# An encoder trunk in fp32 on one Trainium2 core: the first products behind one turned block of x, every second low part on GpSimd, the first norm's squares on VectorE

## Chip, cores, metric

One core of a Trainium2 chip. The time of a kernel is the device time of one launch in microseconds; three runs of the kernel before were timed, and one more was profiled.

## What is computed

A two-layer encoder trunk on 256 tokens of width 1024, fp32. Each layer adds half a SwiGLU block, a mixer (attention of two kinds in the even layer, neighbourhood attention in the odd one) and another half SwiGLU block, each behind an RMS norm:

```python
def rms_norm(x, g):
    y = x * lax.rsqrt(jnp.mean(x * x, axis=-1, keepdims=True) + EPS)
    return y * g
def swiglu(h, w_gate, w_up, w_down):
    return (jax.nn.silu(h @ w_gate) * (h @ w_up)) @ w_down
for layer in range(2):
    x = x + 0.5 * swiglu(rms_norm(x, ffn1_norm[layer]), ffn1_w_gate[layer], ...)
    x = x + mixer(rms_norm(x, mix_norm[layer]), ...)
    x = x + 0.5 * swiglu(rms_norm(x, ffn2_norm[layer]), ffn2_w_gate[layer], ...)
return rms_norm(x, final_norm)
```

The change touches only the very first of these products, `h @ w_gate` on its first 512 columns, and the norm ahead of it.

## The kernel before

The 256 tokens are two tiles (`tt` 0 and 1) of 128 rows. A product needs x turned, so that its width lies on the partitions: eight blocks of 128 columns (`k` 0 to 7) for each tile. Every fp32 operand of a product is split into a high part (rounded to the matmul's format, made by ScalarE) and a low part (what the rounding left, made by VectorE), and a product is three matmuls: high by high, low by high, high by low (`mm`, L407 to L409). For the turned x the two parts are `th` (`part_h`, L447) and `tl` (`part_l`, L452), with the norm's gain on them. For weights they are `hi` (`high_part`, L415) and `lo` (`low_part`, L418). The norm's other factor, one number per row, is applied later, in silu and in the product with the up branch.

Weights are loaded by SyncE's queue into `raw` tiles. `supply` takes the next piece, issues its high part, and keeps its low part back until `low`, at the next `tick` or `supply`. Each product of three matmuls ends in a `tick`, which also steps the spawned tasks (each counts ticks until its next step) and adds `rate` to `due`; when `due` reaches a piece's size, another `supply` is issued ahead of need. The order on every engine is the order in which this program issues, by hand.

The opening is `first_gates`. Four matmuls of zeros warm TensorE (`WARM`). `turn(j)` transposes blocks 2j and 2j + 1 of both tiles into two PSUM banks, `parts(j, banks)` makes their parts and those of the weights, two products' worth of weights (`FIRST`: pieces of 1, 1, 2, 2 and 2 blocks). After `turn(0)` two more matmuls of zeros follow (`FILL`), and then `turn(1)` and its parts stand ahead of the first product:

```python
        parts(0, turn(0))
        for _ in range(FILL):
            self.warm()
        ...
        for j in range(KD // 2):
            if j + 1 < KD // 2:
                banks = turn(j + 1)
                parts(j + 1, banks)
            for k in (2 * j, 2 * j + 1):
                for tt in range(NT):
                    self.mm(ps[tt], now.hT[tt][k], W[k], k == 0, k == KD - 1)
```

`row_rstd`, one task for each tile, squares the two halves of a row on ScalarE with a running sum (L436), adds them on VectorE (L439), scales (L425) and takes the power -1/2 on GpSimd (L427). `SQ_WAIT` is the number of ticks before each starts. The second silu (L594) waits for the second tile's power.

The loads, on SyncE's queue: `mats` (identity and gains), weight block 0, x columns 256 to 512 of both tiles, weight block 1, weight blocks 2 and 3, x columns 512 to 1024, weight blocks 4 to 7; x columns 0 to 256 go through ScalarE's queue.

## Time and profile before

| | us |
|---|---|
| three timed runs: median (lowest, highest) | 966.1 (964.84, 966.28) |
| the profiled execution | 964.81 |
| its span | 963.0 |
| TensorE busy | 950.6 |
| VectorE busy | 694.9 |
| ScalarE busy | 558.0 |
| GpSimd busy | 89.2 |

The span is what the profiler records between the first and the last instruction; the time has 1.8 us more around it. An engine's busy time counts its instructions, so what TensorE lacks to the span is where it stood. The chain that ended last, followed back from the last instruction, says which work set the end.

### The profile page before, as it was taken

Reading aid. Unit: us, or ns where it says so; the run is one execution under the profiler, and the core shown is the slowest. Engines: PE = TensorE matmul, PEld = TensorE weight load, DVE = VectorE, ACT = ScalarE, POOL = GpSimd, SP = SyncE. Lnnn points to the kernel's source line nnn. Section 1 sums busy time; section 2 is a strip of 40 time slices with the busy share of each in tenths; the row PEclk is TensorE's granted clock in tenths of the full one; section 3 lists DMA queues with packets and bytes.
Section 4 is the critical chain, followed back from the end, with each engine's and each line's share of the span. In section 5 each row is a group of like instructions: output and inputs, shape, how many; then the busy total and the mean of one; then the engine's idle time right before and its main releaser. Section 6 shows DMA issues by size and latency. Waiting matters only on the chain.

```text
span 963.0 us, 12839 instructions
## 1 busy us (share of the span) xinstructions
PE 950.6 (99%) x4803; PEld 803.8 (83%) x4803; DVE 694.9 (72%) x1103; ACT 558.0 (58%) x967; POOL 89.2 (9%) x152
## 2 busy tenths in 40 slices
PE   9999999999999999999999999999999999999997
PEld 6888998877878888988888899888878888889886
DVE  6665679778866655787866558889877776655987
ACT  7554556477776545565554445447877575545551
POOL 1030000063420000000000000005130000000001
PEclk9999999999999999999999999999999999999999
DMA  8665565643425744755456556563634356555642
GB/s 285 195 238 185 175 219 178 216 132 89 131 88 201 235 154 131 240 217 207 149 192 207 174 161 220 191 243 132 187 113 135 129 195 201 188 152 182 208 172 80
DMA packets 82367, 171.64 MB, mean 178 GB/s; under 512 B 3712, under 2 KB 25216, under 8 KB 82304
## 3 DMA queue, kind: packets, MB, share of 16 engines
q1 hardware_dynamic: 81728, 170.23, 53.9%
q8 instruction: 37, 0.61, 0.3%
q10 hardware_dynamic: 576, 0.59, 0.2%
q14 instruction: 26, 0.21, 0.1%
HBM read 169.76 MB, written 1.05 MB: 177 GB/s over the span
## 4 chain that ended last, share of the span: by engine, by line
PE 91%; DVE 4%; ACT 2%; POOL 1%; issue 1%; DMA 1%; POOLq 0%; ACTq 0%; DVEq 0%
PE pj L407 14%; PE pj L409 14%; PE pj L408 14%; PE s L409 12%; PE s L407 12%; PE s L408 11%; PE tp L484 3%; PE o L815 2%; PE o L408 1%; PE o L409 1%; PE o L407 1%; PE tp L894 1%; DVE lo L418 1%; PE tp L462 1%; PE s L830 1%
## 5 line engine op out<-in xcount | busy, mean ns | idle before, releaser
L418 DVE TENSOR_TENSOR lo<-raw,hi 128x1024 fp32r<-128x1024 f32 (+2 forms) x388 | 383.2, 1011 | 122.5 <-ACT hi L415 119.0
L415 ACT ACTIVATE hi<-raw 128x1024 fp32r<-128x1024 f32 (+2 forms) x388 | 328.0, 877 | 150.2 <-PE pj L409 101.7
L407 PE MATMUL pj<-hi,th 128*128 128x512 f32 (+1 forms) x512 | 198.1, 387 | 0.0
L409 PE MATMUL pj<-hi,tl 128*128 128x512 f32 (+1 forms) x512 | 192.9, 377 | 0.0
L408 PE MATMUL pj<-lo,th 128*128 128x512 f32 (+1 forms) x512 | 192.7, 376 | 0.1
L407 PE MATMUL s<-hi,th 128*128 128x512 f32 (+1 forms) x400 | 152.2, 380 | 0.0
L409 PE MATMUL s<-hi,tl 128*128 128x512 f32 (+1 forms) x400 | 149.4, 373 | 0.0
L408 PE MATMUL s<-lo,th 128*128 128x512 f32 (+1 forms) x400 | 149.0, 373 | 0.0
L409 PEld LDWEIGHTS pj<-hi,tl 128*128 128x128 f32 x512 | 96.1, 188 | 15.5
L407 PEld LDWEIGHTS pj<-hi,th 128*128 128x128 f32 x512 | 96.4, 188 | 13.8 <-issue 0.9
L408 PEld LDWEIGHTS pj<-lo,th 128*128 128x128 f32 x512 | 96.4, 188 | 13.4 <-DVE lo L418 0.5
L409 PEld LDWEIGHTS s<-hi,tl 128*128 128x128 f32 x400 | 75.2, 188 | 11.0
L408 PEld LDWEIGHTS s<-lo,th 128*128 128x128 f32 x400 | 75.4, 189 | 10.4
L407 PEld LDWEIGHTS s<-hi,th 128*128 128x128 f32 x400 | 75.5, 189 | 10.2
L599 DVE SCALAR_TENSOR_TENSOR glu<-pj,rstd,silu 128x512 f32<-128x512 f32 (+1 forms) x48 | 33.6, 701 | 36.8 <-PE pj L409 36.6
L418 DVE TENSOR_TENSOR g_l<-tp,g_h 128x384 fp32r<-128x384 f32 (+1 forms) x48 | 29.0, 604 | 22.4 <-ACT g_h L415 22.4
L427 POOL TENSOR_TENSOR rstd<-var,mhalf 128x1 f32<-128x1 f32 (+2 forms) x16 | 15.2, 949 | 311.2 <-DVE var L425 311.1
L407 PE MATMUL s<-hi,g_h 128*128 128x512 f32 (+1 forms) x108 | 42.8, 396 | 0.0
L415 ACT ACTIVATE g_h<-tp 128x384 fp32r<-128x384 f32 (+1 forms) x48 | 25.3, 526 | 29.1 <-PE tp L484 19.0
L409 PE MATMUL s<-hi,g_l 128*128 128x512 f32 (+1 forms) x108 | 42.0, 389 | 0.0
L408 PE MATMUL s<-lo,g_h 128*128 128x512 f32 (+1 forms) x108 | 41.9, 388 | 0.0
L447 ACT ACTIVATE th<-tp,mats 128x128 fp32r<-128x128 f32 x88 | 25.1, 371 | 28.4 <-PE tp L462 25.8
(381 smaller groups left out, 1382.0 us busy)
## 6 DMA issues: line engine op xcount, KB each, us to landing
raw<-in_ffn_w_down SPq DMA_DIRECT2D x44, 1024.0 KB, 5.0
raw<-in_ffn_w_up SPq DMA_DIRECT2D x32, 1024.0 KB, 5.2
raw<-in_ffn_w_gate SPq DMA_DIRECT2D x30, 1024.0 KB, 5.3
raw<-in_ffn_w_gate SPq DMA_DIRECT2D x16, 768.0 KB, 4.5
raw<-in_ffn_w_up SPq DMA_DIRECT2D x16, 768.0 KB, 4.8
raw<-in_odd_w_qkv SPq DMA_DIRECT2D x12, 1024.0 KB, 5.3
raw<-in_even_w_in SPq DMA_DIRECT2D x4, 1024.0 KB, 5.2
raw<-in_even_w_out SPq DMA_DIRECT2D x8, 512.0 KB, 5.8
```

What stands on the lines that cost most here:

```text
L407: mm(ps, h, wh, start=first, stop=False)
L408: mm(ps, h, wl, start=False, stop=False)
L409: mm(ps, l, wh, start=False, stop=last)
L415: self.nc.scalar.activation(hi, src, AF.Copy)
L418: self.nc.vector.tensor_tensor(lo, src, hi.bitcast(F32), op=ALU.subtract)
L427: nc.gpsimd.tensor_tensor(r[:, :n], v[:, :n], self.mhalf[:, :n], op=ALU.pow)
L447: self.nc.scalar.activation(hi, tb[:, j * P : j * P + P], AF.Copy, scale=gain)
L462: nc.tensor.transpose(tb[:, j * P : (j + 1) * P], self.x[tt][:, b * P : (b + 1) * P], self.ident)
L484: self.nc.tensor.transpose(tb[:, i * P : (i + 1) * P], src[:, i * P : (i + 1) * P], self.ident)
L599: nc.vector.scalar_tensor_tensor(m[:, :w], u[:, :w], self.now.r[tt], s[:, :w], op0=ALU.mult, op1=ALU.mult)
L815: self.nc.tensor.matmul(O[64 * s : 64 * s + 64, i * P : i * P + P], v(b0 + i, s, kc), pT[s][:, i, kc, :], start=(kc == 0), stop=(kc == 1),)
L830: nc.tensor.matmul(S[:, i, :], q, kz[s], start=True, stop=False)
```

## The change

`first_gates` issues the first pair of products (block 0, both tiles) right behind the warming matmuls; the second `turn` and its parts come behind them, and each later `turn` one pair of products behind an even block. `parts` now issues the weights' high parts first, then for each block the turned parts of both tiles; of its two low parts the first goes to VectorE, the second to GpSimd. `first_rstd` takes the place of `row_rstd` here: VectorE squares and sums with `tensor_tensor_reduce`, scale and epsilon included, and GpSimd takes the power. Its two steps are `SQ_GAP` ticks apart. Weight block 1 is loaded ahead of x columns 256 to 512 (`n == 2`). `FILLER`, the width of a small constant tile, shrinks by what the new small tiles take.

```diff
--- before.py
+++ after.py
@@ -77,11 +77,12 @@
 
 WARM = 4
 FILL = 2
-SQ_WAIT = [4, 8]
-AHEAD_START = 8
+SQ_WAIT = [5, 8]
+SQ_GAP = 4
+AHEAD_START = 9
 FIRST = [1, 1, 2, 2, 2]
 
-FILLER = 128
+FILLER = 80
 HALF = [slice(0, HD), slice(HD, P)]
 
 ROW = 224
@@ -376,14 +377,14 @@
         if split.made == a:
             self.whole.pop(0)
 
-    def low(self):
+    def low(self, eng=None):
 
         if self.half is None:
             return
         split, sl = self.half
         self.half = None
         hi, lo = split.parts
-        self.low_part(lo[:, sl], split.raw[:, sl], hi[:, sl])
+        self.low_part(lo[:, sl], split.raw[:, sl], hi[:, sl], eng)
         if split.then is not None:
             split.then()
             split.then = None
@@ -414,8 +415,8 @@
     def high_part(self, hi, src):
         self.nc.scalar.activation(hi, src, AF.Copy)
 
-    def low_part(self, lo, src, hi):
-        self.nc.vector.tensor_tensor(lo, src, hi.bitcast(F32), op=ALU.subtract)
+    def low_part(self, lo, src, hi, eng=None):
+        (eng or self.nc.vector).tensor_tensor(lo, src, hi.bitcast(F32), op=ALU.subtract)
 
 
     def rstd(self, ss, n, width):
@@ -438,6 +439,19 @@
         s = self.two.tile([P, 1], F32, tag="s1", name=self.name("s1"))
         nc.vector.tensor_tensor(s, ss[:, 0:1], ss[:, 1:2], op=ALU.add)
         dest[tt] = self.rstd(s, 1, D)[:, 0:1]
+
+    def first_rstd(self, tt, dest):
+
+        v = EPS
+        for i in range(2):
+            sq = self.one.tile([P, 512], F32, tag="sq", name=self.name("sq"))
+            x = self.x[tt][:, i * 512 : i * 512 + 512]
+            old, v = v, self.two.tile([P, 1], F32, tag="first_v", name=self.name("v"), bufs=4)
+            self.nc.vector.tensor_tensor_reduce(sq, x, x, 1.0 / D, old, ALU.mult, ALU.add, v)
+            yield SQ_GAP
+        r = self.two.tile([P, 1], F32, tag="first_r", name=self.name("r"))
+        self.nc.gpsimd.tensor_tensor(r, v, self.mhalf[:, 0:1], op=ALU.pow)
+        dest[tt] = r
 
     def part_h(self, tb, tt, i, k, j):
 
@@ -555,27 +569,32 @@
             return banks
 
         def parts(j, banks):
-            for tt in range(NT):
-                now.hT[tt] += [self.part_h(banks[tt], tt, 0, 2 * j + i, i) for i in range(2)]
+
             for i in range(2):
-                self.supply()
+                if W[2 * j + i].split.made <= W[2 * j + i].i:
+                    self.supply()
+                if i == 0 and j == 0:
+                    now.hT = [[self.part_h(banks[tt], tt, 0, 0, 0)] for tt in range(NT)]
+                self.low(nc.gpsimd if i == 1 else nc.vector)
+            for i in range(2):
+                k = 2 * j + i
                 for tt in range(NT):
-                    self.part_l(banks[tt], tt, 0, 2 * j + i, i, now.hT[tt][2 * j + i])
-                self.low()
-
-        parts(0, turn(0))
+                    if k > 0:
+                        now.hT[tt].append(self.part_h(banks[tt], tt, 0, k, i))
+                    self.part_l(banks[tt], tt, 0, k, i, now.hT[tt][k])
+
+        banks = turn(0)
         for _ in range(FILL):
             self.warm()
+        parts(0, banks)
         self.due = -AHEAD_START * RATE[0]
         for tt in range(NT):
-            self.spawn(self.row_rstd(tt, now.r), SQ_WAIT[tt])
-        for j in range(KD // 2):
-            if j + 1 < KD // 2:
-                banks = turn(j + 1)
-                parts(j + 1, banks)
-            for k in (2 * j, 2 * j + 1):
-                for tt in range(NT):
-                    self.mm(ps[tt], now.hT[tt][k], W[k], k == 0, k == KD - 1)
+            self.spawn(self.first_rstd(tt, now.r), SQ_WAIT[tt])
+        for k in range(KD):
+            for tt in range(NT):
+                self.mm(ps[tt], now.hT[tt][k], W[k], k == 0, k == KD - 1)
+            if k % 2 == 0 and k + 2 < KD:
+                parts(k // 2 + 1, turn(k // 2 + 1))
         return ps
 
     def ffn(self):
@@ -1274,7 +1293,7 @@
             warm = self.little([P, 1], "warm")
             nc.scalar.activation(warm, zeros[:, 0:1], AF.Silu)
             for n in range(len(FIRST)):
-                if n == 1:
+                if n == 2:
                     load_x(nc.sync, 256, 512)
                 if n == 3:
                     load_x(nc.sync, 512, D)
```

What this does to the order is shown at three places. `tp` and `pj` are PSUM banks with transposed x, `s` the banks of the products, `x_85` and `x_86` the two tiles, `zeros` the warming matmuls' operand.

TensorE from the two warming matmuls behind the first transposes on, before:

```order
L1253 LDWEIGHTS zeros
L1253 MATMUL o_148<-zeros 128x512
L1253 LDWEIGHTS zeros
L1253 MATMUL o_150<-zeros 128x512
L554 MATMUL pj_152<-mats,x_85 128x128 x2
L554 MATMUL pj_153<-mats,x_86 128x128 x2
L407 MATMUL s_112<-hi_134,th_120 128x512
L408 MATMUL s_112<-lo_135,th_120 128x512
L409 MATMUL s_112<-hi_134,tl_121 128x512
L407 MATMUL s_113<-hi_134,th_126 128x512
L408 MATMUL s_113<-lo_135,th_126 128x512
L409 MATMUL s_113<-hi_134,tl_127 128x512
```

and now:

```order
L1272 LDWEIGHTS zeros
L1272 MATMUL o_120<-zeros 128x512
L1272 LDWEIGHTS zeros
L1272 MATMUL o_122<-zeros 128x512
L408 MATMUL s_112<-hi_126,th_129 128x512
L409 MATMUL s_112<-lo_127,th_129 128x512
L410 MATMUL s_112<-hi_126,tl_130 128x512
L408 MATMUL s_113<-hi_126,th_132 128x512
L409 MATMUL s_113<-lo_127,th_132 128x512
L410 MATMUL s_113<-hi_126,tl_133 128x512
L568 MATMUL pj_158<-mats,x_85 128x128 x2
L568 MATMUL pj_159<-mats,x_86 128x128 x2
```

The transposes of the second pair of blocks went behind the first six matmuls.

GpSimd from its first instruction on the data, before:

```order
L1257 MEMSET mhalf_82 128x128
L427 ISA
L427 TENSOR_TENSOR rstd_239<-var_237,mhalf_82 128x1
L427 TENSOR_TENSOR rstd_292<-var_290,mhalf_82 128x1
L1221 CAST m_394<-mats 128x128
```

and now:

```order
L1276 MEMSET mhalf_82 128x80
L419 ISA
L419 TENSOR_TENSOR lo_139<-raw_100,hi_138 128x512
L419 TENSOR_TENSOR lo_167<-raw_104,hi_166 128x512
L419 TENSOR_TENSOR lo_212<-raw_108,hi_211 128x512
L419 TENSOR_TENSOR lo_260<-raw_110,hi_259 128x512
L453 TENSOR_TENSOR r_293<-v_246,mhalf_82 128x1
L453 TENSOR_TENSOR r_310<-v_288,mhalf_82 128x1
L1240 CAST m_388<-mats 128x128
```

Four low parts of weights stand ahead of the two powers.

VectorE at the end of the first 48 matmuls' parts, from the last pair of turned blocks on, before:

```order
L439 TENSOR_TENSOR s_62_235<-ss_194 128x1
L425 TENSOR_SCALAR var_237<-s_62_235 128x1
L452 SCALAR_TENSOR_TENSOR tl_257<-pj_250,mats,th_256 128x128
L452 SCALAR_TENSOR_TENSOR tl_263<-pj_251,mats,th_262 128x128
L418 TENSOR_TENSOR lo_271<-raw_110,hi_270 128x512
L452 SCALAR_TENSOR_TENSOR tl_260<-pj_250,mats,th_259 128x128
L452 SCALAR_TENSOR_TENSOR tl_266<-pj_251,mats,th_265 128x128
L418 TENSOR_TENSOR lo_271<-raw_110,hi_270 128x512
L439 TENSOR_TENSOR s_81_288<-ss_247 128x1
L425 TENSOR_SCALAR var_290<-s_81_288 128x1
L418 TENSOR_TENSOR lo_303<-raw_132,hi_302 128x1024
L418 TENSOR_TENSOR lo_316<-raw_132,hi_315 128x1024
```

and now:

```order
L450 ISA sq_245,v_246<-x_85,v_198 128x512
L450 ISA v_246 128x1
L419 TENSOR_TENSOR lo_260<-raw_110,hi_259 128x512
L466 SCALAR_TENSOR_TENSOR tl_266<-pj_251,mats,th_265 128x128
L466 SCALAR_TENSOR_TENSOR tl_270<-pj_252,mats,th_269 128x128
L466 SCALAR_TENSOR_TENSOR tl_274<-pj_251,mats,th_273 128x128
L466 SCALAR_TENSOR_TENSOR tl_278<-pj_252,mats,th_277 128x128
L450 ISA sq_287,v_288<-x_86,v_240 128x512
L450 ISA v_288 128x1
L419 TENSOR_TENSOR lo_298<-raw_124,hi_297 128x1024
L419 TENSOR_TENSOR lo_313<-raw_124,hi_312 128x1024
```

The last square and the read of its sum stand behind the last turned low parts, where the sum and the scaling stood.

## Rows read from the trace of the kernel before

**Rows 1.** The profile's page, its first part: busy us of each engine, share of the span, instructions.

```profile
PE 950.6 (99%) x4803; PEld 803.8 (83%) x4803; DVE 694.9 (72%) x1103; ACT 558.0 (58%) x967; POOL 89.2 (9%) x152
```

**Rows 2.** Four stretches of a table of the span by stages: start and end (us), length, then the busy time of TensorE (PE), its weight loads (PEld), VectorE (DVE), ScalarE (ACT) and GpSimd (POOL) with their instructions, the granted TensorE clock (1.00 is full), the busy share of the DMA engines and GB/s.

```profile
1.45:9.00 7.55, 6.85 (x18) 3.38 (x19) 2.63 (x7) 4.63 (x12) 0.00 (x0) 1.00 0.93 293
9.00:20.00 11.00, 11.00 (x54) 9.06 (x53) 9.26 (x24) 10.32 (x27) 1.87 (x2) 1.00 0.92 292
...
25.00:100.00 75.00, 75.00 (x345) 62.06 (x345) 46.37 (x55) 37.90 (x52) 8.40 (x24) 1.00 0.60 197
100.00:950.00 850.00, 845.77 (x4331) 719.26 (x4331) 624.73 (x997) 499.04 (x871) 72.59 (x116) 1.00 0.53 175
```

**Rows 3.** The chain that ended last, pieces in order of time, from 5 to 20 us: start, length (both us), what. `tp L554` and `pj L554` are transposes, `s L407` to `L409` the products.

```profile
5.13 0.69 PE tp L554 x2
...
6.89 0.85 PE pj L554 x4
7.74 0.43 PE s L407
...
8.60 0.43 PE s L409
9.02 0.28 PE s L407
9.30 0.23 PE s L408
...
11.15 0.44 PE tp L554 x4
...
14.35 0.44 PE pj L554 x4
...
19.37 0.24 PE s L409
```

**Rows 4.** The same chain from 20 to 24 us, and under it TensorE's own timeline there (start, length, engine, line, operation, output and inputs).

```profile
20.38 0.04 ACT silu L594
...
20.96 1.06 ACT hi L415
...
22.05 1.24 DVE lo L418
...
22.84 0.39 PE L407 MATMUL pj<-hi,th 128*128 128x512 f32 x1
23.33 0.50 PE L408 MATMUL pj<-lo,th 128*128 128x512 f32 x1
```

**Rows 5.** Loads of the opening. Above, issues on SyncE's queue in the timeline (start, length of the issue, xcount). Below, answers of the DMA view for the issues at 1.17, at 1.65, at 2.59 and at about 3.0: operands, queue, count, KB each, us from issue to landing.

```profile
1.17 0.42 SPq L322 DMA_DIRECT2D raw<-in_ffn_w_gate  x1
1.65 0.90 SPq L1267 DMA_DIRECT2D x<-in_x  x2
2.59 0.91 SPq L322 DMA_DIRECT2D raw<-in_ffn_w_gate  x2
11.67 3.64 SPq L322 DMA_DIRECT2D raw<-in_ffn_w_up  x2
...
raw<-in_ffn_w_gate SPq DMA_DIRECT2D x1, 256.0 KB, 3.7
...
x<-in_x SPq DMA_DIRECT2D x1, 128.0 KB, 3.7
...
raw<-in_ffn_w_gate SPq DMA_DIRECT2D x1, 256.0 KB, 5.0
...
raw<-in_ffn_w_gate SPq DMA_DIRECT2D x1, 512.0 KB, 5.8
```

**Rows 6.** ScalarE and VectorE in the opening, from the timeline: its table load, a high part, four turned high parts; a turned low part and a low part on VectorE.

```profile
1.65 1.28 ACT L1275 ACT_TABLE_LOAD   x1 [1.65 <-PEq L1313]
6.38 0.63 ACT L415 ACTIVATE hi<-raw 128x512 fp32r<-128x512 f32 x1
8.16 1.12 ACT L447 ACTIVATE th<-pj,mats 128x128 fp32r<-128x128 f32 x4
6.52 0.35 DVE L452 SCALAR_TENSOR_TENSOR tl<-tp,mats,th 128x128 fp32r<-128x128 f32 x1 [0.68 <-ACT th L447]
9.83 0.69 DVE L418 TENSOR_TENSOR lo<-raw,hi 128x512 fp32r<-128x512 f32 x1 [0.17 <-ACT hi L415]
```

**Rows 7.** GpSimd: its two powers in the opening, with the VectorE row that gives the first one its operand and the one that runs beside the second, and its two operations of 128x512 with two inputs, at the kernel's end.

```profile
15.02 0.15 DVE L425 TENSOR_SCALAR var<-s 128x1 f32<-128x1 f32 x1
15.32 0.55 POOL L427 TENSOR_TENSOR rstd<-var,mhalf 128x1 f32<-128x1 f32 x1 [14.39 <-DVE var L425]
18.62 2.36 DVE L418 TENSOR_TENSOR lo<-raw,hi 128x1024 fp32r<-128x1024 f32 x2
18.68 1.57 POOL L427 TENSOR_TENSOR rstd<-var,mhalf 128x1 f32<-128x1 f32 x1 [2.81 <-DVE var L425]
...
950.85 1.75 POOL L1198 TENSOR_TENSOR shi<-x,last_gain 128x512 f32<-128x512 f32 x1 [167.15 <-DVE x L537]
955.52 1.29 POOL L1198 TENSOR_TENSOR shi<-x,last_gain 128x512 f32<-128x512 f32 x1 [1.36 <-DVE x L537]
```

**Rows 8.** VectorE's squares with a running sum, at the kernel's end.

```profile
950.75 0.69 DVE L1188 CUSTOM_DVE_ANT_0 sq<-x 128x512 f32<-128x512 f32 x1
...
952.09 1.05 DVE L1188 CUSTOM_DVE_ANT_0 sq<-x,v 128x512 f32<-128x512 f32 x1
```

## The prediction

> **What bounds the kernel now.** I read the busy times first, then a table by stage, then the chain of waits through the first 24 us, then the DMA, ScalarE, VectorE and GpSimd rows around it. TensorE is busy for 950.6 us, 99% of the span of 963.0 [rows 1]. By stage, from 25 to 100 us it is busy all the time and from 100 to 950 us it is idle for 4.2 us, in work the diff leaves in its order [rows 2]. What the change can reach is the opening. There the rows say four things.
>
> First, TensorE hardly waits for data even there. The second tile's transposes start at 5.13, when its x has landed; then come two warming matmuls, four more transposes at 6.89, and the first product at 7.74 [rows 3].
>
> Second, it is slow there. The column of the granted clock reads 1.00 in every stretch [rows 2], but the first three products take 0.43 us each and from 9.30 each takes 0.23 [rows 3]. For 512 columns, 0.43 us is the lower of the two levels (1.2 GHz) and 0.23 close to the upper (2.4 GHz); the spacing decides, and it says that the level rose at about 9.1 after TensorE had worked without a break since 5.13.
>
> Third, after the rise TensorE is packed: from the fifth product at 9.30 to the end of the 45th at 19.61 stand 41 products and two groups of four transposes of 0.44, so (10.31 - 0.88) / 41 = 0.23 for each product [rows 3]. No row in that stretch shows TensorE waiting for ScalarE or VectorE.
>
> Fourth, there is one wait behind it: ScalarE does its second silu at 20.38, so the next high part starts at 20.96, its low part at 22.05, and a product that stood ready at 23.07 (0.23 after the product at 22.84) starts at 23.33 [rows 4]. That is 0.26 us.
>
> The profiled execution took 964.81 us: the span of 963.0 and 1.8 around it. The three timed runs are 964.84, 966.10 and 966.28. With the profiled one, two runs lie near 964.8 and two near 966.2, mean 965.5; the median given, 966.1, is 1.3 above the profiled run. About 0.2%, or 1.9 us, is what a measurement of this kernel can tell from no change.
>
> **The change, part by part.**
>
> *First products ahead of the second group of transposes.* The 48 products, 16 transposes and six warming matmuls all remain. The first product can start when the second warming matmul ends, at 6.89, if its inputs are there. raw_98 lands at 1.17 + 3.7 = 4.87 [rows 5], its high part takes 0.63 [rows 6] and ends near 5.5. The turned part of the first half follows the transposes that end at 5.82, plus about 0.4: both before 6.9. The low part (0.69) ends near 6.4 and the two turned low parts at about 6.7 and 6.9 [rows 6]; they are needed at 7.3, 7.8 and 9.0. So the product moves from 7.74 to 6.89, and the 0.85 us of transposes move behind six products.
>
> What is that worth? Before, from 6.89: transposes 0.85, three products at 0.43 (1.28 by the rows), one of 0.28, 44 at 0.23 (10.12) and two groups of transposes (0.88): the end is at 20.30. Now, if the level rises at the same moment: 4.95 products fit between 6.89 and 9.02, then 43.05 at 0.23 are 9.90 and three groups of transposes 1.32: 20.24. The gain is 0.06 us: the transposes cost half as much later, but so would the products they displace. TensorE had no hole to fill; the warming matmuls had filled it.
>
> *The order of the loads.* raw_100 (256 KB) goes ahead of the x columns 256 to 512 (two of 128 KB) and nothing else moves on SP's queue. Before, this place in the queue landed between 1.65 + 3.7 = 5.4 and 5.7, and the later place at 2.59 + 5.0 = 7.6 [rows 5]. ScalarE's in-order queue now meets raw_100 before it can do the next turned parts, which are needed only at 9.7; the x columns are wanted by the second transposes at 9.26. Both are 1.6 us early or more. raw_104 keeps its place and lands at about 8.8 (issued at 3.0, 5.8 to landing): its high parts end at 9.5 and 10.05, the turned parts behind them at 10.3 and 10.55, and the products need them at 11.08 and 11.77. Cost: zero, with 0.8 us of cover.
>
> *Every second low part on GpSimd.* Four operations of 128x512 with two inputs from SBUF move off VectorE (0.69 each). GpSimd has this shape twice, at 1.75 and 1.29 us [rows 7]; I take 1.75. Each starts 0.15 after its high part: 6.95, 10.2, 12.85 and 15.85, and ends at 8.7, 11.95, 14.6 and 17.6. With the products at the places worked out above they are needed at 9.93, 13.1, 16.3 and 19.1. The smallest cover is 1.15 us, so TensorE waits only if one takes over 2.9. Three of them also free the raw buffers for which SP's next 1 MB loads wait: the first goes out at 11.95 instead of 11.67 [rows 5], the two others earlier than before, and the first high part that reads it has its place on ScalarE only at about 17.8. Zero.
>
> *The squares on VectorE.* Four squares leave ScalarE. It was 94% busy from 9 to 20 us (10.32 of 11.00 [rows 2]), but TensorE did not wait for it, so this frees nothing on the path. On VectorE each costs 0.69 [rows 8]; the four low parts that left pay for it. What counts is when the last one ends. The last transposes now stand behind the fifth pair of products and end at 16.10, where they ended at 14.79 before. The turned parts of that bank alternate between ScalarE and VectorE now, one waiting for the other, four steps of about 0.35 with 0.17 between: the last ends near 18.3. Then the square to 18.95, and GpSimd's power starts at 19.1. That operation took 0.55 once and 1.57 once; the slow one ran beside VectorE's 1024-wide low parts [rows 7], and that neighbour is there again from 19.0. So 1.57, to 20.7, and the second silu starts at 20.75 where it started at 20.38. The high part, the low part and the product at 23.33 all slip with it: **+0.4 us**. With 0.55 the cost is nothing; with a square of 1.05, as one took beside GpSimd [rows 8], it is +0.75.
>
> *The rest.* The start of the feed (AHEAD_START 9 for 8) makes one split a place earlier on ScalarE and VectorE until about 80 us, where TensorE has no idle time; the order is then the old one. The tiles' padding offsets the new small tiles. Zero.
>
> Sum: -0.06 + 0.4, or +0.34: 965.15 on the profiled run, and on the middle of the four runs, 965.5, which I take: **965.9 us**.
>
> On GpSimd a rule speaks against the change. Before, GpSimd's first such operation started at 15.32, right behind the operand ready at about 15.17, and took 0.55 [rows 7]: no delay for a first call. The Trainium skill, GPSIMD Engine Reference, section "Instruction dispatch", says that the first call to a freshly loaded kernel pays about 6 us of loading that no profile row shows. By the row the first low part ends at 8.7 and costs nothing. By the page, paid at that call, it would end near 14.7 and TensorE would lose about 4.8 us, an estimate from that page: 970.3.
>
> **The rivals.**
>
> *A, the forecast: TensorE's work is only put in another order.* -0.06 to +0.75 us: from 964.8 - 0.06 to 966.3 + 0.75 with the runs' own spread. Chance 0.75.
>
> *B, faster: the level rises earlier*, since real products stand where transposes stood. If it rises 1.28 us after the first product, as before, that is at 8.17: three slow products, then 45 at 0.23 and 1.32, end 19.84, a gain of 0.46. The most this can give is the upper level from 6.89 on: 48 x 0.23 + 1.32 = 12.36, end 19.25, a gain of 1.05. From 964.8 less 1.05, or 963.8, to 966.3 less 0.46. For it: a us at the lower level costs 0.47 (0.20 of each 0.43), so the two groups of runs, 1.4 us apart, look like a rise some 3 us apart. Against: transposes and warming matmuls kept TensorE working before too. Chance 0.15.
>
> *C, slower: GpSimd and VectorE get in each other's way.* The power took 2.85 times as long beside a low part [rows 7]. A low part stretched like that takes 1.29 x 2.85 = 3.7 us, over the 2.9 where it decides. TensorE then waits 0.75 at the second pair of products, 0.5 at the sixth and 1.0 at the eighth, and the two powers come last and add 0.7: +3.0, 968.5 us. Against: VectorE's work beside the first two is mostly on PSUM, not on two SBUF inputs. The Trainium skill, GPSIMD Engine Reference, section "Key points", names just that pair, GpSimd beside a VectorE instruction with two SBUF inputs, as the contended one; the trace agrees, with 1.57 beside 0.55. Chance 0.08.
>
> *D, slower: GpSimd's first operation is late* by a one-time loading, at the second pair. It decides beyond 1.2 us late, and 0.2% is lost from 3.1 us on. The only loading in the rows, ScalarE's table, takes 1.28 [rows 6] and would cost 0.05; the power's start 0.15 behind its operand speaks for none. Chance 0.02.
>
> **How the numbers follow.** A lies almost wholly within 0.2% of 966.1. B counts as faster only with most of its gain and a run of the lower group: 0.08, and A adds 0.03 through the runs' spread. C and D are slower beyond 0.2%, mostly: 0.08. So 0.11 faster, 0.81 same, 0.08 slower. The range runs from B's lower end, 963.8, but for a little, to A's upper end, 967.05, and a little over: 963.9 to 967.2. C and D stay outside.
>
> **What would show it.** In the changed profile the first product should stand at 6.9 in the chain, six products ahead of the second transposes; the first 48 should end within 0.3 us of 20.2; GpSimd should show four low parts of 1.3 to 1.8 us with no TensorE wait behind them; the second silu should wait for GpSimd's power until about 20.7, and the one product near 23.3 should stand later. A drop to 0.23 spacing well before 9 us would show B; a TensorE gap released by a low part on GpSimd would show C, one of several us at the second pair D. A first product still at 7.7 would mean that a load, not the order, had held it.

## The result and the profile after

The changed kernel takes **967.03 us** (median of 21 runs, 965.46 to 967.48), the kernel before, on the same chip, 965.59 (21 runs, 964.39 to 966.28). The ratio is 1.0015, with an interval of 1.0009 to 1.0021: the change costs 1.4 us. The profiled execution of the changed kernel took 966.8 us, its span is 964.8.

The page's first part, the answer to [rows 1]:

```profile
PE 951.9 (99%) x4803; PEld 804.0 (83%) x4803; DVE 695.8 (72%) x1103; ACT 557.0 (58%) x959; POOL 94.3 (10%) x156
```

The table by stage (columns as in [rows 2]):

```profile
1.45:9.00 7.55, 6.75 (x16) 3.26 (x17) 1.82 (x5) 4.30 (x9) 1.28 (x1) 1.00 0.94 310
9.00:20.00 11.00, 11.00 (x52) 8.83 (x51) 9.08 (x22) 7.43 (x19) 5.67 (x4) 1.00 0.87 280
20.00:25.00 5.00, 4.63 (x20) 3.17 (x19) 4.02 (x6) 4.82 (x7) 2.36 (x2) 1.00 0.76 250
25.00:100.00 75.00, 75.00 (x344) 62.02 (x345) 46.62 (x55) 37.62 (x51) 7.27 (x24) 1.00 0.60 201
100.00:950.00 850.00, 845.76 (x4332) 719.01 (x4330) 623.73 (x995) 500.94 (x873) 72.58 (x116) 1.00 0.54 175
```

From 25 us on it is the old kernel: TensorE busy all the time to 100 us, and 845.76 after it where [rows 2] have 845.77. ScalarE fell from 10.32 to 7.43 between 9 and 20 us, GpSimd rose from 1.87 to 5.67: work moved as meant. The loss is in the opening. Everything behind 26 us stands 1.52 us later than before (read from VectorE rows that both kernels have; 1.5 to 1.85 to the end).

The chain that ended last, from 6 to 25 us (start, length, what), the answer to [rows 3] and [rows 4]:

```profile
6.94 0.43 PE s L408
...
9.50 0.85 PE pj L568 x4
10.35 0.33 PE s L408
10.68 0.23 PE s L409
...
13.18 0.23 PE tp L568 x2
...
15.15 0.68 DVE sq L450
...
16.64 1.69 DVE lo L419
18.33 0.27 DVE tl L466
18.60 0.02 issue
18.63 0.38 ACT th L461
19.00 0.02 issue
19.03 0.29 DVE tl L466
...
19.55 0.74 DVE sq L450
...
20.39 1.50 POOL r L453
...
21.90 0.02 ACT silu L613
...
23.57 1.24 DVE lo L419
24.81 0.04 issue
24.85 0.50 PE pj L409
```

Two things are to be seen. The first product does stand at 6.94, six products of 0.43 ahead of the second transposes; but those still take 0.85 and the spacing falls to 0.23 only behind 10.35: in this execution the level rose 1.3 us later than before ([rows 3]: between 9.02 and 9.30). And the chain leaves TensorE. Before, it ran through products to 19.61; now it leaves them behind the transposes of 13.18 and runs over turned parts and two squares to a low part of 1.69 on VectorE, and from there over turned parts, the last square, the power and the second silu to a product at 24.85 that stood at 23.33 [rows 4].

VectorE there, from the timeline (start, length, engine, line, operation; `ANT_0` is the square):

```profile
12.46 0.69 DVE L419 TENSOR_TENSOR lo<-raw,hi 128x512 fp32r<-128x512 f32 x1
...
15.88 0.75 DVE L450 CUSTOM_DVE_ANT_0 sq<-x,v 128x512 f32<-128x512 f32 x1
...
16.55 1.78 DVE L419 TENSOR_TENSOR lo<-raw,hi 128x512 fp32r<-128x512 f32 x1
...
20.23 2.36 DVE L419 TENSOR_TENSOR lo<-raw,hi 128x1024 fp32r<-128x1024 f32 x2
```

And GpSimd, its four low parts and the two powers, the answer to [rows 7]:

```profile
6.88 1.28 POOL L419 TENSOR_TENSOR lo<-raw,hi 128x512 fp32r<-128x512 f32 x1 [5.99 <-ACT hi L416]
9.71 1.28 POOL L419 TENSOR_TENSOR lo<-raw,hi 128x512 fp32r<-128x512 f32 x1 [1.55 <-ACT hi L416]
12.66 1.62 POOL L419 TENSOR_TENSOR lo<-raw,hi 128x512 fp32r<-128x512 f32 x1 [1.68 <-ACT hi L416]
15.97 1.81 POOL L419 TENSOR_TENSOR lo<-raw,hi 128x512 fp32r<-128x512 f32 x1 [1.68 <-ACT hi L416]
17.74 1.00 POOL L453 TENSOR_TENSOR r<-v,mhalf 128x1 f32<-128x1 f32 x1
20.39 1.49 POOL L453 TENSOR_TENSOR r<-v,mhalf 128x1 f32<-128x1 f32 x1 [1.64 <-DVE v L450]
```

GpSimd's low part of block 7 (15.97) and VectorE's of block 6 (16.55) meet. GpSimd's takes 1.81 in place of 1.28, **VectorE's 1.78 in place of 0.69** [rows 6]. The ends tell more than these lengths. GpSimd's began beside VectorE's square (15.88 to 16.63) and ended at 17.78, 1.15 behind it; VectorE's low part ended at 18.33, 0.55 behind that. One pair earlier VectorE's low part had begun first (12.46): it took its usual 0.69, and GpSimd's beside it (12.66) took 1.62 and ended 1.13 behind it. The two engines look as if they took turns, each of these operations running to its end while the other waits. That is read from the ends; no run tried it by itself.

TensorE pays at three places (its timeline; `s` are products of the gate branch, `pj` from 21.06 on those of the up branch, the up products below; the starts tell, a product that does not wait follows the last at 0.23):

```profile
18.04 0.40 PE L408 MATMUL s<-hi,th 128*128 128x512 f32 x1
18.39 0.50 PE L409 MATMUL s<-lo,th 128*128 128x512 f32 x1
18.73 0.42 PE L410 MATMUL s<-hi,tl 128*128 128x512 f32 x1
...
21.06 0.39 PE L408 MATMUL pj<-hi,th 128*128 128x512 f32 x1
21.51 0.50 PE L409 MATMUL pj<-lo,th 128*128 128x512 f32 x1
...
24.16 0.39 PE L408 MATMUL pj<-hi,th 128*128 128x512 f32 x1
24.85 0.50 PE L409 MATMUL pj<-lo,th 128*128 128x512 f32 x1 [0.31 <-DVE lo L419]
```

The first two up products before, in the same view:

```profile
20.12 0.39 PE L407 MATMUL pj<-hi,th 128*128 128x512 f32 x1
20.34 0.39 PE L408 MATMUL pj<-lo,th 128*128 128x512 f32 x1
```

Each of the three is the first product that reads a certain low part (`L409`). At 18.39 it waited for the late low part (16.55 to 18.33) and followed at 0.35 instead of 0.23; at 21.51 it waited for the first of VectorE's 1024-wide low parts, behind the late square, and followed at 0.45; at 24.85 it waited for the chain above, 0.69 where it was 0.49 [rows 4]. The product behind one that waited follows at 0.34 and not at 0.23, which adds 0.11 at the first two places; the third had that before too. So 0.23 + 0.33 + 0.20 = **0.76 us of new waits**, and the lower level for 1.3 us more, at 0.47 us each (0.20 of every 0.43), makes 0.61: together 1.37 of the 1.52.

### The profile page after: what moved, and what is told of

Same layout as the page of the kernel before. It is cut to its first block, busy times and chain, and to the rows that moved or that the text cites. A ratio compares the mean times of both kernels' runs of the same rounds, so it can differ in the third digit from the quotient of the medians.

```text
span 964.8 us, 12842 instructions
## 1 busy us (share of the span) xinstructions
PE 951.9 (99%) x4803; PEld 804.0 (83%) x4803; DVE 695.8 (72%) x1103; ACT 557.0 (58%) x959; POOL 94.3 (10%) x156
## 3 DMA queue, kind: packets, MB, share of 16 engines
HBM read 169.76 MB, written 1.05 MB: 177 GB/s over the span
## 4 chain that ended last, share of the span: by engine, by line
PE 90%; DVE 4%; ACT 2%; POOL 1%; issue 1%; DMA 1%; POOLq 0%; ACTq 0%; DVEq 0%
PE pj L408 14%; PE pj L410 14%; PE pj L409 14%; PE s L408 11%; PE s L410 11%; PE s L409 11%; PE tp L498 3%; PE o L834 2%; DVE lo L419 1%; PE o L409 1%; PE o L410 1%; PE o L408 1%; PE tp L913 1%; PE tp L476 1%; PE s L849 1%
## 5 line engine op out<-in xcount | busy, mean ns | idle before, releaser
L409 PE MATMUL pj<-lo,th 128*128 128x512 f32 (+1 forms) x512 | 192.8, 376 | 0.4 <-DVE lo L419 0.3
L409 PE MATMUL s<-lo,th 128*128 128x512 f32 (+1 forms) x400 | 149.4, 373 | 0.0
L409 PEld LDWEIGHTS pj<-lo,th 128*128 128x128 f32 x512 | 96.4, 188 | 14.1 <-DVE lo L419 1.2
L410 PEld LDWEIGHTS s<-hi,tl 128*128 128x128 f32 x400 | 75.4, 188 | 11.2
L409 PEld LDWEIGHTS s<-lo,th 128*128 128x128 f32 x400 | 75.6, 189 | 10.7 <-DVE lo L419 0.4
L618 DVE SCALAR_TENSOR_TENSOR glu<-pj,rstd,silu 128x512 f32<-128x512 f32 (+1 forms) x36 | 25.2, 701 | 29.3 <-PE pj L410 29.2
L409 PE MATMUL s<-lo,g_h 128*128 128x512 f32 (+1 forms) x108 | 41.9, 388 | 0.0
L428 POOL TENSOR_TENSOR rstd<-var,mhalf 128x1 f32<-128x1 f32 (+2 forms) x14 | 13.1, 933 | 293.5 <-DVE var L426 293.4
```

Of the source, the lines that this page charges most:

```text
L409: mm(ps, h, wl, start=False, stop=False)
L410: mm(ps, l, wh, start=False, stop=last)
L428: nc.gpsimd.tensor_tensor(r[:, :n], v[:, :n], self.mhalf[:, :n], op=ALU.pow)
L618: nc.vector.scalar_tensor_tensor(m[:, :w], u[:, :w], self.now.r[tt], s[:, :w], op0=ALU.mult, op1=ALU.mult)
```

## The experiments

The theories. **W**: the new waits cost it, because the two engines slow each other in the last pair of blocks, and the last square, its power and the second silu come late. **L**: the new order makes the level rise late. **R**: the level's rise differs from execution to execution whatever the kernel. **P** came up after the first four: the memory layout. **V**: in the new order VectorE alone cannot make both low parts of a pair in time. **W1**, **W2** and **S** are explained where they are tested. Each run was timed beside the kernel before (medians 965.1 to 965.5 in the four batches). "Later at 26 us" is against the profile of before, as above.

**1. Squares back on ScalarE**, the rest of the change kept.

```diff
-            self.spawn(self.first_rstd(tt, now.r), SQ_WAIT[tt])
+            self.spawn(self.row_rstd(tt, now.r), SQ_WAIT[tt])
```

> The changed kernel with one part undone: the first norm's squares back on ScalarE (order, load order and GpSimd's low parts stay). Theory W (the loss is waits: GpSimd's and VectorE's low parts stretch each other, the last square ends late, the second silu waits for GpSimd's power): the power is ready before the products end, the second silu follows the last product by 0.1 us, VectorE's last low part ahead of the up branch is on time; about 1.0 us faster than the changed kernel, so +0.4 against before. Rival L (the new order makes TensorE's level rise later, at about 10.4 instead of 9.1, worth 0.65 us; only the silu is a wait): about 0.6 faster than the changed kernel, +0.8 against before, and 0.43 us products until beyond 10 us in the profile.

970.97 us, ratio 1.0061 (1.0048 to 1.0073). At 26 us it stands exactly where before stood; the loss builds up afterwards (1.2 us at 195, 3.9 at 656, 5.4 at the end). The edit drops small tiles, so every later tile lies lower: no word on the squares, and the reason for theory P.

**2. The order alone**: squares on ScalarE and all low parts on VectorE.

```diff
-                self.low(nc.gpsimd if i == 1 else nc.vector)
+                self.low()
...
-            self.spawn(self.first_rstd(tt, now.r), SQ_WAIT[tt])
+            self.spawn(self.row_rstd(tt, now.r), SQ_WAIT[tt])
```

> The changed kernel with both engine moves undone: squares on ScalarE, all low parts on VectorE; only the order of TensorE's work, of the parts and of the loads is left. W: equal to before within 0.3 us, since the order only exchanges transposes for products. L: +0.65 against before, with the level rising at about 10.4 in the profile.

972.03 us, 1.0072 (1.0058 to 1.0086); 2.4 later at 26 us, the rest builds up later as in 1.

**3. The last pair's low part back on VectorE.**

```diff
-                self.low(nc.gpsimd if i == 1 else nc.vector)
+                self.low(nc.gpsimd if i == 1 and j < 3 else nc.vector)
```

> The changed kernel with GpSimd's fourth low part (weight block 7) back on VectorE; the first three stay on GpSimd. W: VectorE's low part of block 6 falls from 1.78 to 0.69 and the one of block 7 adds 0.6, so the last square ends about 0.5 us earlier, and the power runs without a stretched neighbour ahead of it: 0.5 faster than the changed kernel, +0.9 against before. L: at most 0.3 faster, +1.1.

966.33 us, 1.0010 (1.0001 to 1.0018). VectorE's last pair and last square, from the timeline:

```profile
15.90 1.29 DVE L419 TENSOR_TENSOR lo<-raw,hi 128x512 fp32r<-128x512 f32 x2
...
18.42 0.74 DVE L450 CUSTOM_DVE_ANT_0 sq<-x,v 128x512 f32<-128x512 f32 x1
```

GpSimd's second power behind them:

```profile
19.25 1.49 POOL L453 TENSOR_TENSOR r<-v,mhalf 128x1 f32<-128x1 f32 x1 [2.25 <-DVE v L450]
```

VectorE makes both low parts in 1.29, less than it took for one beside GpSimd. The square, the power and the second silu (20.77) stand close to where the prediction put them, two of the three waits are gone, the third stays (0.71). So the profile shows what W said. The time does not tell W from L: it is 1.1 above before, where W expected 0.9 and L 1.1, and only 0.3 less than the change lost.

**4. GpSimd's low parts alone**, in the kernel before (`low` and `low_part` take the engine as in the change).

```diff
-                self.low()
+                self.low(nc.gpsimd if i == 1 else None)
```

> The kernel before with one part of the change alone: every second low part of the opening on GpSimd. W: the low parts beside GpSimd's stretch, but the squares are on ScalarE and the power stays early: 0 to +0.3 against before; a VectorE low part of 1.2 to 1.8 us beside a GpSimd one should be in the profile. L: 0.

965.16 us, 1.0001 (0.9992 to 1.0010): nothing. In the old order VectorE is all but done with its low part when GpSimd begins. VectorE in the timeline:

```profile
17.46 0.69 DVE L418 TENSOR_TENSOR lo<-raw,hi 128x512 fp32r<-128x512 f32 x1 [0.17 <-ACT hi L415]
...
18.59 0.75 DVE L439 TENSOR_TENSOR s<-ss 128x1 f32<-128x1 f32 x1
```

GpSimd beside it:

```profile
18.03 1.30 POOL L418 TENSOR_TENSOR lo<-raw,hi 128x512 fp32r<-128x512 f32 x1 [1.24 <-ACT hi L415]
...
19.61 1.57 POOL L427 TENSOR_TENSOR rstd<-var,mhalf 128x1 f32<-128x1 f32 x1 [0.28 <-DVE var L425]
```

The low parts take 0.69 and 1.30. What does meet GpSimd's is a one-column addition: it took 0.75 and ended at 19.34, together with GpSimd's (19.33). In the profile of before it took 0.15:

```profile
18.26 0.15 DVE L439 TENSOR_TENSOR s<-ss 128x1 f32<-128x1 f32 x1
```

**5 and 6. The same as 1 and 2 with the tiles where they were**: the edits above and

```diff
-FILLER = 80
+FILLER = 128
```

> As sq_on_act (the changed kernel with the squares back on ScalarE), with the small constant tile at its old width of 128, so that every tile behind the pool of small tiles lies where it lay in the kernel before. In sq_on_act the opening ended level with before and the 5.4 us were lost evenly in later stages, at products 0.24 us apart instead of 0.23. Theory P (the place of the tiles in SBUF, 192 bytes lower, cost that): the later loss is gone, W: +0.3 against before. If the place does not matter: +5.8 again.

> As order_alone (only the order of products, parts and loads; all low parts on VectorE, squares on ScalarE), with the constant tile at its old width. In order_alone the opening ended 2.4 us late with the level rising at about 11.6, with TensorE waiting at three products for VectorE's parts; less 0.47 us for each us of the later rise that is +1.2. Theory V (in the new order VectorE cannot make both low parts of a pair in time): +1.2 against before. W as first stated (the order is neutral): 0. L: +0.65.

With squares on ScalarE 965.6 us, 1.0005 (0.9996 to 1.0013): no loss that can be told. GpSimd's low parts take 1.28 to 1.30 and VectorE's 0.69: with no squares on VectorE its low part is again done first. The order alone: 967.16, 1.0020 (1.0011 to 1.0029). It has waits of 0.67, 0.58 and 0.48 at 17.8 to 21.8, since ScalarE's high parts come behind its squares and VectorE has both low parts of a pair to make: this order needs GpSimd's help. V expected a loss of 1.2 for that reason; 1.85 came.

**7. The squares alone on VectorE**, in the kernel before (`first_rstd` added, and what follows).

```diff
-            self.spawn(self.row_rstd(tt, now.r), SQ_WAIT[tt])
+            self.spawn(self.first_rstd(tt, now.r), SQ_WAIT[tt])
...
-FILLER = 128
+FILLER = 80
```

> The kernel before with the squares alone moved to VectorE (constant tile at 80, which the new small tiles make up for). VectorE's busy time from 9 to 20 us would go from 9.3 to about 11.4 of 11.0. W: VectorE becomes the bound of the opening, low parts and the power come late: +0.5 to +1.0 against before. L: 0.

966.02 us, 1.0008 (0.9999 to 1.0017). The last square ends at 19.9, the power (20.00, 1.47) holds the second silu to 21.51, and the two up products follow at 0.31 and 0.67: 0.37 us by the profile, 0.71 by the medians, which the interval does not tell from nothing.

**8. The shift alone**: the kernel before with its tiles 192 bytes lower.

```diff
-FILLER = 128
+FILLER = 80
```

> The kernel before with nothing changed but the width of the constant tile, 80 instead of 128, so that all tiles behind it lie 192 bytes lower in each partition. P: +4 to +6 us, with the opening unchanged. If not the place, but the chip or the order made the two slow kernels slow: 0.

970.17 us, 1.0054 (1.0042 to 1.0067): +4.9 us from 48 floats less in a tile of constants. Theory P holds. The change itself keeps the layout.

**9. The changed kernel again**, unchanged but for an empty line, so that its lines count one higher.

> The changed kernel itself once more, for a second profile of it and a second time. If the rise of TensorE's clock level differs from execution to execution whatever the order (theory R), this profile's rise stands anywhere between 8.0 and 11.6 us and only by chance at the 10.4 of the first one, while the waits behind GpSimd's last low part come back: VectorE's low part of block 6 at 1.5 to 1.8 us, the second power ending at 21.5 or later. If the new order makes the rise late (theory L), it stands at 10.2 to 10.6 again. Time 966.4 to 967.3 by both.

966.5 us, 1.0013 (1.0004 to 1.0022). Its TensorE in the opening:

```profile
7.37 0.63 PE L410 MATMUL s<-lo,th 128*128 128x512 f32 x1
7.79 0.47 PE L411 MATMUL s<-hi,tl 128*128 128x512 f32 x1
```

The next products stand at 8.11, 8.34 and 8.57. The level rose at 8.1, earlier than in the profile of before, and 2.3 us earlier than in the first profile of the same kernel. So the new order alone does not make the rise late, as L had it; that the rise differs from execution to execution, R, fits. The waits are back (0.35, 0.47, 0.71), VectorE's low part takes 1.78 again; at 26 us it is 0.52 later than before.

**10. The squares two and three products sooner.** W1: the place of the last square costs; W2: the slowing costs wherever the squares stand.

```diff
-SQ_WAIT = [5, 8]
+SQ_WAIT = [3, 5]
```

> The changed kernel with its four squares started two and three products sooner (SQ_WAIT 3 and 5 for 5 and 8), so that the last square stands ahead of VectorE's low part of block 6 and not behind the last turned low parts; memory is laid out as before. Theory W1 (the place of the last square is what costs: it holds the power and the second silu): the second power ends by 19.5 us, the second silu no longer waits for it, the loss against the kernel before falls from 1.4 to 0.3 to 0.7 us. Theory W2 (the two engines' slowing of each other costs, wherever the squares stand): the low part of block 6 still takes 1.3 us or more, the turned low parts behind it come late and TensorE waits for them; the loss stays at 1.1 to 1.6 us.

967.74 us, 1.0028 (1.0017 to 1.0039), the slowest with the layout kept. VectorE in the timeline:

```profile
13.25 1.76 DVE L419 TENSOR_TENSOR lo<-raw,hi 128x512 fp32r<-128x512 f32 x1
...
17.03 1.87 DVE L450 CUSTOM_DVE_ANT_0 sq<-x,v 128x512 f32<-128x512 f32 x1
...
18.83 0.68 DVE L419 TENSOR_TENSOR lo<-raw,hi 128x512 fp32r<-128x512 f32 x1
```

GpSimd's third and fourth low part:

```profile
12.73 1.75 POOL L419 TENSOR_TENSOR lo<-raw,hi 128x512 fp32r<-128x512 f32 x1 [2.10 <-ACT hi L416]
17.06 1.29 POOL L419 TENSOR_TENSOR lo<-raw,hi 128x512 fp32r<-128x512 f32 x1 [2.59 <-DVE v L450]
```

The slowing went along: the low part of block 4 takes 1.76 now, and the last square 1.87 beside GpSimd's low part, so VectorE's low part of block 6 starts at 18.83, and TensorE's product of 18.52 is followed only at 19.57. Here too VectorE's operations end 0.53 and 0.55 behind GpSimd's (15.01 behind 14.48, 18.90 behind 18.35). W1's gain came (both powers end by 19.92, the second silu no longer waits), W2's loss was more. Neither gave the size.

**11 and 12. Without the two warming matmuls**: number 5, and the kernel before, with

```diff
-FILL = 2
+FILL = 0
```

> The changed kernel with the squares on ScalarE, memory laid out as before (FILLER 128), and the two warming matmuls behind the first transposes left out. They cover the time in which the first turned parts are made, so TensorE's first product can start at about 6.3 in place of 6.9, at most 0.6 us sooner, but TensorE stands for about 0.5 us. If the level rises at the same moment for all that: 0.3 to 0.6 us below the same kernel with the two matmuls (965.6), so about 965.1. If it rises later, each us later costs 0.47: 965.6 to 966.5.

> The kernel before with those two warming matmuls left out and nothing else. The second transposes follow the first at 5.8 and the first product can start near 6.9 in place of 7.74: 0.4 to 0.8 us less if the rise of the level stays where it is, so 964.5 to 965.0; 965.3 to 966.3 if the rise comes later for it.

965.45 us, 1.0005 (0.9996 to 1.0014), and 966.25, 1.0011 (1.0002 to 1.0019). Number 12's first product starts at 7.10, 0.64 sooner, but the level rose at 10.4 in its profile. No gain in either.

**13 to 16. The hole ahead of the second transposes filled.** The waits make 0.76 us, the medians say 1.44 and 1.38. R: the rest is the level, later in the median by chance or tendency; S: it is in every execution, elsewhere. Three more warming matmuls at the start, in the kernel before, in the change, in number 5 and in number 3:

```diff
-WARM = 4
+WARM = 7
```

> The kernel before with seven warming matmuls at the start in place of four, so that TensorE has work until the x of both tiles has landed at about 5.1 us. If the level then rises sooner and at the same moment in every execution (R), the times fall by 0.5 to 1.5 us and their range of 1.9 us narrows to under 1. If the rise does not depend on that hole, 964.5 to 966.5 as before.

> The changed kernel with the same three warming matmuls more. With a level that rises early and alike in both, theory R expects it 0.6 to 1.0 us above before_warm (the waits that the profiles show), theory S 1.2 to 1.6 us above it.

> The changed kernel with the squares on ScalarE, memory laid out as before, and the same three warming matmuls more. Its waits were about as small as those of the kernel before, so by both theories it should stand within 0.4 us of before_warm; below it if the order of the products gains what it was meant to.

> The changed kernel with the last of the four low parts back on VectorE, and the same three warming matmuls more. If the slowing of the two engines in the last pair is what made the waits, it stands 0.2 to 0.5 us above before_warm and 0.4 to 0.7 below change_warm; if the level made the difference between the two, the same as change_warm.

965.6 us (1.0001, 0.9993 to 1.0010), 966.52 (1.0009, 1.0000 to 1.0018), 965.97 (1.0004, 0.9995 to 1.0013) and 965.45 (0.9999, 0.9990 to 1.0008). The times neither fell nor narrowed: filling the hole did not fix the rise (6.6 to 9.2 in these four). But the profiles of the first two rose alike, at 9.0 and 9.2, and make a clean pair: the change stands 0.38 us later at the first up product and 0.93 at 26 us; the medians differ by 0.92. That is R's 0.6 to 1.0, though the intervals of two such medians do not exclude 1.2. Number 16 stands 1.07 below number 14, where W expected 0.4 to 0.7 from the waits at the first two places; in number 3 the same edit had taken off only some 0.3. So far do medians of 11 runs lie apart; the profiles of both show the same two waits gone.

**The profiles side by side.** Rise: where the spacing falls from 0.43 to 0.23. A, B, C: distance from the product that stands ready to the next, behind block 6's low part, at the first and at the second up product (0.23 is no wait). "Sum" adds 0.47 for each us of rise behind 9.05, each wait over before's, and 0.11 for each product restarted that was not before.

| kernel | rise | A | B | C | sum | later at 26 us |
|---|---|---|---|---|---|---|
| before | 9.05 | 0.23 | 0.23 | 0.49 | 0 | 0 |
| changed | 10.35 | 0.35 | 0.45 | 0.69 | 1.37 | 1.52 |
| changed, again | 8.1 | 0.35 | 0.47 | 0.71 | 0.35 | 0.52 |
| 3, last pair on VectorE | 9.1 | 0.23 | 0.24 | 0.71 | 0.36 | 0.41 |
| 4, low parts alone | 11.15 | 0.23 | 0.23 | 0.49 | 0.99 | 0.93 |
| 5, squares on ScalarE | 8.55 | 0.35 | 0.39 | 0.38 | 0.05 | 0.13 |
| 7, squares alone | 10.45 | 0.23 | 0.31 | 0.67 | 1.03 | 1.13 |
| 10, squares sooner | 11.4 | 1.05 | 0.44 | 0.42 | 2.28 | 2.41 |
| 13, before, 7 warming | 9.0 | 0.23 | 0.23 | 0.49 | -0.02 | 0.47 |
| 14, changed, 7 warming | 9.2 | 0.35 | 0.44 | 0.71 | 0.84 | 1.40 |
| 15, number 5, 7 warming | 7.3 | 0.34 | 0.39 | 0.42 | -0.51 | 0.16 |
| 16, number 3, 7 warming | 6.6 | 0.23 | 0.25 | 0.71 | -0.80 | -0.23 |

Rise and waits account for the opening within 0.2 us. In 13 to 16 the transposes start at 5.7 in place of 5.13 behind the longer warming, which the sum leaves out; there it falls short by 0.5 to 0.7 alike. Of the profiles with four warming matmuls, numbers 1, 2, 6, 8, 11 and 12 among them, the nine with the new order have a median rise of 9.1 (8.1 to 11.6), the five with the old one 10.4 (8.2 to 11.2): with such a scatter that speaks neither for L nor for an earlier rise by the order. No kernel run here beats the kernel before beyond its interval.

## Why the prediction was wrong

It said 965.9, a change that cannot be told from none (its own sum, 965.5 + 0.34, gives 965.8); it came to 967.0 and a loss of 1.4 us that can be told. That the time lies inside the range is luck: the range's upper end was made of the runs' spread and of a slower square, and neither is what happened.

- *What bounds the kernel, the base of 965.5*: right. 965.59 is the median of 21 runs, and behind 26 us nothing changed.
- *The order, -0.06*: nearly. In the clean pair (13, 14) 0.38 is lost up to the first up product, of which the wait at A makes 0.22; +0.16 is left for the order, and some 0.09 of that is the 0.2 us by which 14's level rose later. Its condition, that the level rises at the same moment, can't be counted on in a single profile: the same kernel rose at 10.35, 8.1 and, with more warming, 9.2. Rival B, an earlier rise by the order, has no support.
- *The loads, zero*: right; the first product stood at 6.94, and no product waited for a load. The cover is gone, though, where the level rises early: in number 9 the chain that ended last goes back to a weight load that landed at 11.27, with ScalarE's high parts right behind it.
- *Every second low part on GpSimd, "Zero"*: **this step failed.** The lengths on GpSimd were as taken (1.28 to 1.81 for 1.75), no product waited for one of them, and by themselves they cost nothing that can be told (number 4). What was left out is that GpSimd's holds up what VectorE does beside it: the sum kept VectorE's low part at 0.69 and it took 1.78. That made the waits at A and, for the most part, at B, 0.56 us in the first profile; with the last pair back on VectorE (numbers 3 and 16) A is gone and B is down to 0.24 and 0.25.
- *Rival C* had the right neighbours, the wrong victim and the wrong price. It stretched a GpSimd operation by a factor and asked from which length TensorE waits for that, 2.9; the longest of GpSimd's was 1.81. The price fell on VectorE, 1.09 us at one instruction, with everything queued behind it: four turned low parts, the last square, two 1024-wide low parts. By the ends, the price of a meeting is not a factor but what is left of the other engine's operation, at most its 1.28. The sentence against it looked at the first two pairs; the last one decided. The Trainium skill, GPSIMD Engine Reference, section "Key points", names the pair, a GpSimd operation beside a VectorE instruction with two SBUF inputs; the rows agree, 1.78 for 0.69 on VectorE and 1.81 for 1.28 on GpSimd.
- *The squares and the late power, +0.4*: the mechanism was right, its size and share were not. The second silu did wait for the power (21.90), the product at 23.33 did slip. At that place it cost 0.20 to 0.22; alone the move cost 0.37 at both up products (number 7). And the squares did a second thing that was not seen: they put VectorE's low part behind them, into GpSimd's. Without squares on VectorE (number 5) the two low parts do not meet; without GpSimd's last one (number 3) there is nothing to meet. By their waits the two moves cost nothing (number 4) and 0.37 us (number 7) alone, and 0.76 together in the new order. Both together in the old order, and the squares with all low parts on VectorE in the new one, were not run.
- *Rival D*: right to give it little. GpSimd's first low part began at 6.88, right behind its high part, and took 1.28; the loading of some 6 us that the Trainium skill, GPSIMD Engine Reference, section "Instruction dispatch", puts at the first call to a freshly loaded kernel does not show in this trace. GpSimd had stood idle for 5.99 us ahead of that low part, and longer ahead of the first power before; whether a loading ran unseen in that time no run here shows.

Put into the sum, +0.16 for the order and 0.22 + 0.32 + 0.22 for the three waits make 0.92, the 0.93 of the clean pair's profiles from which the 0.16 was taken. Another 0.2 lies outside the span: over the timed runs, time less span has a median of 2.0 in the six kernels with squares on VectorE and low parts on GpSimd, 1.8 in the nine others that keep the layout; why was not found. Of the measured 1.44 and 1.38 that leaves about 0.3 us open. By means in place of medians the loss is 1.36 and 1.24, with a standard error of about 0.17, so that 0.1 to 0.3 is left, hardly more than the scatter. The level's rise is wide enough for it, but it was not shown that the changed kernel rises later on average.

## What to carry to other kernels

When work moves to GpSimd, price the engine that stays too: look what VectorE does at that moment in the new order, and put the two operations one behind the other, with both queues behind them. Two moves that cost little alone can meet: redraw the timeline with both before calling either zero. And where one profile's clock level rises is one draw; compare two kernels at an equal rise, or by the time of the waits.

## What the runs showed of the hardware

- Where a VectorE operation on 512 columns (a low part or a square) met a low part of 512 columns on GpSimd that had begun ahead of it, or within 0.03 us, it took 1.76 to 1.87 in place of 0.69 to 0.75, and a one-column addition 0.75 in place of 0.15. It ended 0.53 to 0.55 us behind GpSimd's, the addition 0.01. Where VectorE's had begun 0.2 us ahead, it took 0.69 and GpSimd's 1.62. Turned low parts, which read a PSUM bank, took 0.34 and 0.35 beside GpSimd's first low part (6.88 to 8.16), no more than elsewhere.
- The granted-clock column reads 1.00 throughout the opening, but by the spacing of the products the level rose anywhere from 6.6 to 11.6 us, in one and the same kernel at 8.1 and 10.35, and neither the order of the first products nor three more warming matmuls fixed it. At 0.47 us of time for each us, 5.0 us of it make 2.3 us; the 21 runs of either kernel spread over 1.9 and 2.0.
- With the same program and its tiles 192 bytes lower, the kernel took 4.9 us more. The products of one later stage, from 138 to 178 us, by line (last two numbers ahead of the idle time: busy us, mean ns), in the shifted kernel:

```profile
L408 PE MATMUL pj<-lo,g_h 128*128 128x512 f32 x12 | 4.7, 394 | 0.0
L409 PE MATMUL pj<-hi,g_l 128*128 128x512 f32 x12 | 4.7, 394 | 0.0
```

The same lines have 389 and 390 in the kernel before. The loss does not build up evenly: by VectorE's rows 1.3 us come from 120 to 200 us and none from 200 to 400, the rest in a few stretches behind 400. What in the placement does it was not tried.
